# A planner's estimate of TensorE that counts a fixed time for each matrix product

## The chip, the cores and the metric

The kernel runs on one core of one Trainium2 chip. The time is device microseconds from the first to the last instruction of one execution. All weights lie in HBM at the start; the inputs and outputs are those of the reference, in float32.

## The reference

One sequence of 256 tokens with 1024 features goes through two blocks. The first has three residual steps; the second has two layers that carry the tokens and a context stream of 256 rows beside them.

```python
def first_block(...):
    x = x + parallel_mixer(rms_norm(x, mix_norm), w_in, conv_w, lb, hgrn_norm, w_out)
    x = x + memory_cross_attention(rms_norm(x, xattn_norm), rms_norm(mem, mem_norm), w_q, w_kv, w_o)
    x = x + hierarchical_moe(rms_norm(x, ffn_norm), w_group, b_group, w_expert, b_expert, w_gate, w_up, w_down)
    return rms_norm(x, final_norm)

def second_block(x, c, ctx, c_ctx, norm_g, w_ada, ...):
    for l in range(2):
        shift, scale, gate = split(silu(c) @ w_ada[l] + b_ada[l], 3)
        h = rms_norm(x, norm_g[l]) * (1 + scale) + shift
        hc = rms_norm(ctx, norm_g[l]) * (1 + scale_c) + shift_c
        # each of h and hc @ w_in[l]: queries, keys, values of three kinds of attention, z, gates
        o_na, o_mla, o_diff = ...           # the tokens look at tokens and context
        x_new = x + gate * merge_branches(o_na, o_mla, o_diff, z, gm, w_br[l], w_out[l])
        if l == 0:
            ctx = ctx + gate_c * merge_branches(the context's own three branches)
        x = x_new
    return x
```

The router of the mixture of experts takes `softmax(t @ w_group + b_group)` and `t @ w_expert + b_expert` (4 + 16 columns) and picks one of four groups and two of its four experts for each token.

## The kernel before

Most products take float32 operands as two float32r parts: `hi` carries the leading bits, `lo` the rest, and a product of two matrices is three products on TensorE (hi·hi, hi·lo, lo·hi), 128 rows deep and 256 or 512 columns wide. The weights come in units of 512 KB (for instance 4 slices of 128 rows by 256 columns). SP issues the load into a raw tile `w`, ACT copies it into its leading part `wh`, DVE subtracts to make `wl`. A unit of `gemm_t` (token rows out, 256 columns) is 4 slices x 2 token tiles x 3 parts = 24 products for each stream.

The program is one straight list of instructions for each engine. Its order is set while it is built: every part of the computation is a generator (`Fiber`), and `run()` takes, again and again, the fiber that can go on earliest by an estimate, `max(its ready time, self.E["pe"])`, and at equal times the one of the smallest priority number. `self.E` holds the estimated end of each engine's list; `_op` moves it on by a cost, `_pe` computes that cost for products and transposes, `act`, `tt`, `ts`, `stt` do so for ACT and DVE. The estimate also tells `soon()` whether a fiber should let others go first, and `splitter()` when a weight may be split. The build is repeated: the order in which weight units were used in one build is the order in which the next one loads them. On the chip the engines then wait for each other through semaphores, in exactly this order; the estimate itself doesn't run there.

Names that matter below:

- `mm` (line 365) emits a product, `tr` (line 370) a transpose on TensorE against the identity in `csts`; `act` (378) an ACT operation, `tt` (388), `ts` (393, 395), `stt` (400, 402), `red` (407, 409) DVE operations.
- `layer(l, ...)`: one layer of block 2. Its last step, `out`, multiplies the merged branches by `w_out_2` in units of 256 columns and adds them to the tokens' residual `X`: a product with the gate into a temporary `t`, then two additions to `X`. `layers` starts layer 1's context stream as soon as layer 0's context is through (`hidden(C, 1, 1, ...)`); the tokens follow (`rest()`: wait for layer 0, then `hidden(X, 1, 0, ...)`, at the high priority `CRIT`). `hidden` squares and sums `X`, takes the inverse root, scales (one tile on ACT, one on DVE), and `to_T2` makes 16 transposes in four groups and evacuates each group: a scale and shift on DVE or ACT, `hi` on ACT, `lo` on DVE. Layer 1's first projections are 8 units of the context alone; those of the tokens need `hidden`.
- `moe`: the router's logits are products with `wrh`, `wrl` (line 365, 20 rows out), evacuated by ACT (`t<-p,cols 20x256`) and transposed back (`tr`, `p<-csts,t 20x20`). The softmax and the choice follow on DVE.
- `prepare` (priority 8, the lowest): 16 small copies within HBM that lay out the window's bias (`toep`, line 949). ACT's queue issues them, so ACT stands still while an issue lasts.

Of the kernel before, what the change touches and what calls it, by code (L numbers as in the profile page):

```python
# [11 lines left out]
F32R = mybir.dt.float32r  # L12
# [9 lines left out]
EPS = 1e-6  # L22
NEG = -1e30
NE = 16
CAP = 64

# ---------------------------------------------------------------- layout of the packed small operands
# [72 lines left out]
# ---------------------------------------------------------------- program order  # L100
# [5 lines left out]
class Fiber:  # L106
# [10 lines left out]
    def ready(self, eng="pe"):  # L117
        """when the fiber's last result can be used by an engine."""
        return self.t + (0 if self.eng is None else self.SELF[eng] if self.eng == eng else
                         self.HOP_PE if eng == "pe" else self.HOP)  # L120
# [6 lines left out]
class Tiles:  # L127
    """[128, n, w] held as tiles of per entries each."""
# [12 lines left out]
class Core:  # L141
    """Emits the program. Each part of the computation is a generator; run() interleaves them by an
    estimate of when the engines are free, so that one part's products fill another's waits."""
# [3 lines left out]
    # per phase: weights loaded, weights split (each as two parts); the rest of the large tiles are the fibers'  # L147
    WEIGHTS = {"start": (5, 4), "router": (19, 2), "moe": (9, 2), "moe2": (7, 2), "l0": (4, 3), "l1": (3, 4)}
    QUOTA = {"start": {}, "router": {("l", "M"): 3}, "moe": {}, "moe2": {}, "l0": {}, "l1": {}}
    UNITS, OPEN = 6, 5  # L150
    PAR = {1: 1.0, 2: 1.87, 4: 3.6}
# [51 lines left out]
    # ---- generators  # L203
# [47 lines left out]
    # ---- memory  # L251
# [28 lines left out]
    def alloc_t(self, n, w, dt=F32):  # L280
        """[128, n, w] in as many tiles as it takes."""
        per = min(n, 1024 // w)
        ts = []
        for i in range(0, n, per):
            m = min(per, n - i)
            x = yield from self.alloc("M" if m * w > 512 else "S", [128, m, w], dt)
            ts.append(x)
        return Tiles(ts, per)

    def alloc_2(self, n, w):  # L290
        """[128, n, w] twice: leading and trailing parts."""
        hi = yield from self.alloc_t(n, w, F32R)
        lo = yield from self.alloc_t(n, w, F32R)
        return hi, lo
# [12 lines left out]
    def wlimit(self, phase):  # L307
        """the phase's share of the large tiles for weights; what a smaller share gives back is used once it is empty."""
        r, h = self.WEIGHTS[phase]
# [10 lines left out]
    def soon(self, eng="pe"):  # L320
        """other parts first, if what comes would hold up the engine."""
# [16 lines left out]
    # ---- engines  # L338
# [7 lines left out]
    def _pe(self, cycles, rows, par=1.0):  # L346
        """the array runs at its full clock in a tick that follows one with enough columns; par: products side by side."""
# [5 lines left out]
        self._op("pe", cycles * (0.4167 if self.hot else 0.8333) / par)  # L353
# [8 lines left out]
    def mm(self, out, lhsT, rhs, start, stop, par=1.0):  # L362
        n, m = self._n(rhs), self._n(lhsT)
        self._pe(max(n, 2 * m) if rhs.dtype == F32R else max(4 * n, 4 * m), lhsT.shape[0], par)
# [53 lines left out]
    def rsqrt(self, ss, inv_n, n):  # L418
        """1/sqrt(ss*inv_n + EPS) for a [128, n] tile; 1/sqrt(ss) without inv_n."""
# [18 lines left out]
    def hilo(self, hi, lo, src, after=None):  # L438
        """Exact split of src: hi carries its leading bits, lo the rest."""
# [4 lines left out]
    # ---- weights  # L444
# [17 lines left out]
    def _slot(self):  # L462
        """a large tile for weights: the one that was given back first."""
# [10 lines left out]
    def _pump(self):  # L474
        """loads ahead of the products, in the recorded order, as far as the buffers allow."""
# [3 lines left out]
    def splitter(self):  # L479
        """splits ahead of the products; hi: the leading bits of the unit's weights, lo: the rest."""  # L480
# [26 lines left out]
    def wget(self, name, lead, k0, k1, c0, c1, plain=False):  # L507
        """the weights [k0*128:k1*128, c0:c1], [128, k, c]: split, or plain as they are."""
# [66 lines left out]
    def gemm_w(self, name, lead, K, c0, c1, hi, lo, evac):  # L575
        """out[feature, token]: evac(i, psum [128, 2, 256]) for each 256 columns."""
# [19 lines left out]
    def gemm_x(self, name, lead, K, c0, c1, hi, lo, evac, cw=512):  # L596
        """out[token, feature]: evac(i, [psum of tokens 0-127, psum of tokens 128-255], n)."""
# [21 lines left out]
    def gemm_f(self, name, lead, K, c0, blocks, hi, lo, evac, pair=False, base=0, end=2 * T, kev=None):  # L619
        """out[feature, token] in blocks of at most 128 features; blocks: (features, first token), the tokens running to  # L620
        end, of which hi/lo hold those from base; kev: what each entry of hi/lo waits for. evac(block, psum [features, tokens], psum tile), or with pair
        evac(block, psum [128, blocks, tokens], psum tile)."""
# [3 lines left out]
        for b0 in range(0, len(blocks), 2):  # L626
# [12 lines left out]
            for k0 in range(0, kt, 4):  # L639
                w = yield from self.wget(name, lead, k0, k0 + 4, c, c + cw)  # L640
                f = 0
                for j, (fw, t0) in enumerate(bl):
# [4 lines left out]
                    if fw == 32:  # L647
                        # a narrow block's leading and trailing parts side by side, to be added up later
# [4 lines left out]
                        for k in range(4):  # L653
                            # (the product that ends the group writes all of its rows)
# [24 lines left out]
    def gemm_t(self, name, lead, K, c0, c1, hi, lo, streams, evac, cw=256, base=0, kev=None, group=1):  # L679
        """out[token, feature] for both tiles of each stream: evac(i, [psum [128, 2 * cw] for each stream]) for every cw  # L680
        columns; hi/lo hold the tokens from base; kev: what each entry of hi/lo waits for."""
# [31 lines left out]
    def gemm_m(self, name, lead, K, c0, cw, hi, lo, streams, evac, base=0):  # L713
        """out[token, feature], cw columns, the weights held for both tiles of each stream: evac(m, [psum for each stream])."""
# [26 lines left out]
    def gemm_p(self, ps, st, par, units, kt, n=512):  # L741
        """ps[rows of part j] = st(j, k).T @ part j's weights for all parts side by side, the weights as they are;
        units: (name, lead, first column) of each part."""
# [16 lines left out]
    # ---- shared pieces  # L760
# [12 lines left out]
    def norm_rows(self, src, inplace=False):  # L773
        """src / rms, tokens on partitions: two [128, 1024] tiles."""
# [20 lines left out]
    def to_T(self, xs, hi, lo, a=None, b=None, nk=8, at=0, off=0):  # L795
        """transposes xs (two tiles, tokens on partitions) into entries at.. of hi/lo, scaled by columns a, shifted by b."""
# [49 lines left out]
    def add_rows(self, dst, gate=None):  # L846
        """evac for gemm_x: dst += psum (times a gate row)."""
# [14 lines left out]
    # ---- setup  # L862
# [29 lines left out]
    def silu_c(self):  # L892
        """silu of the two conditioning vectors, over and over."""
# [8 lines left out]
    def lower(self):  # L902
        """lower bound of the forget gates: softmax over the layers' rows, its first row."""
# [13 lines left out]
    def prepare(self):  # L917
        """small operands that are needed later: router weights, lambda, the window's bias."""
# [23 lines left out]
        # the window's bias as a function of both columns  # L942
# [12 lines left out]
    # ---- block 1: mixer  # L955
# [195 lines left out]
    def decays(self, A, K, Q, B, KT, qts, made, used):  # L1151
        """level by level: queries and keys times their decays from and to the middle of each block."""
# [29 lines left out]
    # ---- block 1: memory keys and values  # L1182
# [38 lines left out]
    # ---- block 1: cross attention  # L1221
# [78 lines left out]
    # ---- block 1: experts  # L1300
    def moe(self):
# [5 lines left out]
        # router  # L1307
# [96 lines left out]
        # slot numbers of every token as rows, combine weights of every slot as columns  # L1404
# [26 lines left out]
        # tokens beyond an expert's CAP slots, if there are any  # L1431
# [24 lines left out]
    def gained(self, xs):  # L1456
        """the experts' input, tokens on partitions, as leading and trailing parts."""
# [12 lines left out]
    def square(self, m, c):  # L1470
        """the sums of squares of a piece of the residual stream, before and after the final gain."""
# [9 lines left out]
    def gather(self, q, before, hh, hl, pos, C2, cw):  # L1481
        """the rows of four experts' tokens, features on partitions; the slots' weights, two experts side by side."""
# [38 lines left out]
    def experts(self, gat, cw, ups, ys):  # L1521
        """the products with the experts' weights, two experts' slots side by side, one pair after the other."""
        hid = []

        def down(p):
            """the weighted result as leading and trailing parts, slots on partitions."""
# [46 lines left out]
    def hid(self, g, u):  # L1573
        """silu(gate) * up of two experts' slots, features on partitions."""
# [18 lines left out]
    def scatter(self, q, evs, posT, after, piece, pieces):  # L1593
        """token t takes the slots that carry its number."""
# [30 lines left out]
    def overflow(self, hh, hl, over, mxi):  # L1625
        """the dense products of every expert, weighted by over; taken only if an expert's slots ran out."""
# [50 lines left out]
    def final_norm(self, hi, lo):  # L1677
        """the final norm of block 1, and the first layer's norm on top of it: 1/rms of the latter from the sums of squares
        after the gain."""
# [25 lines left out]
    # ---- block 2  # L1705
    def ada(self, l, *evs):
        """shift, scale and gate of layer l for both streams, features on partitions."""
# [42 lines left out]
    def gate_rows(self, l, streams):  # L1750
        """the gates of the streams (0 the tokens, 1 the context) as rows, on every partition."""
# [12 lines left out]
    def hidden(self, src, l, s, hi, lo, inplace=False):  # L1764
        """the modulated, normalised stream s of layer l (0 the tokens, 1 the context) into its half of hi/lo."""
# [10 lines left out]
    def layer(self, l, hi, lo, C, ready, half=None):  # L1776
        """one layer of block 2 on both streams (0 the tokens, 1 the context), the context in columns 0-255 of hi/lo and the
        tokens in 256-511, these from ready on; the last layer takes keys and values alone from the context. The first
        layer has the context alone in hi/lo, which does what it can by itself before the tokens are ready, and half is
        set when the context's residual stream is done."""  # L1780
# [10 lines left out]
        def rope(r, tb, nh, d):  # L1791
            """r [128, m, nh, d] (or [128, m, d], nh None) in place."""
# [19 lines left out]
        def heads(br):  # L1812
            """four tiles of heads, features on partitions, as leading and trailing parts if the scores are taken from these."""
# [15 lines left out]
        def heads_T(raw, np_, nb, dst, d0, gain):  # L1829
            """blocks raw(m, j) of np_ columns, tokens on partitions, into dst[d0 + j]."""  # L1830
# [12 lines left out]
        def sums(n, cols):  # L1843
            """sums of squares of n blocks of columns, to be turned into 1/rms in one go."""
# [3 lines left out]
        def roots(sh, j, inv_n):  # L1848
            """block j's 1/rms, once the other blocks' sums are there too."""
# [868 lines left out]
```

## Time and profile before

| | us |
|---|---|
| median of 3 runs | 1619.11 (1617.6 to 1622.94) |
| span of the profiled execution | 1620.1 |
| PE busy / weight loads busy | 1581.4 / 1333.1 |
| DVE busy / ACT busy | 980.5 / 753.2 |
| mean granted TensorE clock | 0.995 |

PE is TensorE's product side, PEld its weight loads (they run beside the products), DVE the vector engine, ACT the scalar engine. The granted clock is a share of 2.4 GHz; 0.5 is the lower level, 1.2 GHz. In a timeline row the columns are start, duration, engine, line, operation, names out<-in, shape, count, and in brackets the idle time of that engine just before and what ended it. Products overlap in the pipeline, so a row with x2 lasts less than twice a row with x1; the pitch from start to start is what counts.

### The profile page before, as it was taken

To read this page: it belongs to the slowest core of one execution; us is meant where nothing else is said; L and a number is where in the kernel's file an instruction comes from. 1 tells how busy PE (TensorE), PEld (TensorE's weight loads), DVE (VectorE), ACT (ScalarE), POOL (GpSimd) and SP (SyncE) were. 2 spreads that over 40 slices of the span, in tenths; PEclk is the share of its full clock that TensorE was granted. 3 is DMA by queue.
4 is the path that set the end of the run, shared out by engine and by line. 5 is a ranking of instruction groups with operands and counts; after the bars stand their busy time and mean duration, and the time that the engine had idled before them with its cause. 6 is when DMAs were issued, how large, how long until landed. Compare 5 with 4: busy or idle time off the path is not lost.

```text
span 1620.1 us, 28916 instructions
## 1 busy us (share of the span) xinstructions
PE 1581.4 (98%) x11642; PEld 1333.1 (82%) x11642; DVE 980.5 (61%) x2035; ACT 753.2 (46%) x1357; POOL 44.1 (3%) x75
## 2 busy tenths in 40 slices
PE   7999999699999999999999999999999999999998
PEld 6899899663565447998888788888999999989898
DVE  5876557522232246758675463754896776767755
ACT  5535345322522135746653345463464465546652
POOL 0000000000000001011000000000010200000000
PEclk9999999899999999999999999999999999999999
DMA  9667656779998996565314453534755425234441
GB/s 344 225 189 241 221 162 188 237 275 377 383 372 291 353 384 211 170 182 132 104 50 123 128 157 113 166 92 130 234 167 159 118 79 144 69 113 112 144 133 63
DMA packets 233175, 305.31 MB, mean 188 GB/s; under 512 B 17184, under 2 KB 160288, under 8 KB 233040
## 3 DMA queue, kind: packets, MB, share of 16 engines
q1 hardware_dynamic: 222608, 293.11, 56.5%
q0 software_dynamic: 2576, 7.77, 1.7%
q10 hardware_dynamic: 7856, 2.56, 0.8%
q8 instruction: 93, 1.52, 0.4%
q14 instruction: 42, 0.34, 0.1%
HBM read 302.34 MB, written 2.90 MB: 188 GB/s over the span
## 4 chain that ended last, share of the span: by engine, by line
PE 63%; DVE 2%; ACT 1%; DMA 1%; issue 0%; DVEq 0%; ACTq 0%
PE p L365 59%; PE p L370 4%; ACT t L378 1%; DMA w<-in_w_in_dram 1%; DVE t L388 0%; DVE wl L388 0%; DVE t L400 0%; ACT wh L378 0%; DVE t L407 0%; DVE t L409 0%; ACT X L378 0%; DVE t L395 0%; DVE t L393 0%; DVE p L388 0%; DVE X L388 0%
## 5 line engine op out<-in xcount | busy, mean ns | idle before, releaser
L365 PE MATMUL p<-t,wh 128*128 128x256 f32 (+1 forms) x2640 | 560.9, 309 | 0.7 <-DVE t L388 0.7
L365 PE MATMUL p<-wh,t 128*128 128x256 f32 (+2 forms) x2248 | 464.9, 301 | 1.5 <-ACT wh L378 1.2
L388 DVE TENSOR_TENSOR wl<-w,wh 128x1024 fp32r<-128x1024 f32 (+2 forms) x318 | 373.4, 1194 | 133.6 <-ACT wh L378 122.5
L365 PEld LDWEIGHTS p<-t,wh 128*128 128x128 f32 x2640 | 424.1, 190 | 31.0 <-issue 7.8
L378 ACT ACTIVATE t<-p 128x512 f32<-128x512 f32 (+5 forms) x381 | 193.5, 528 | 453.2 <-PE p L365 341.7
L365 PE MATMUL p<-t,wl 128*128 128x256 f32 (+1 forms) x1312 | 399.6, 305 | 0.5 <-DVE wl L388 0.5
L365 PEld LDWEIGHTS p<-wh,t 128*128 128x128 f32 x2248 | 366.3, 192 | 23.9 <-issue 11.0
L378 ACT ACTIVATE wh<-w 128x1024 fp32r<-128x1024 f32 (+2 forms) x318 | 318.7, 1031 | 42.5 <-DMA toep<-in_na_rpb_dram 11.4
L365 PE MATMUL p<-wl,t 128*128 128x256 f32 (+2 forms) x1124 | 335.4, 298 | 2.1 <-DVE wl L388 2.1
L365 PEld LDWEIGHTS p<-t,wl 128*128 128x128 f32 x1312 | 250.0, 191 | 11.8 <-DVE wl L388 0.9
L365 PE MATMUL p<-t,t 128*64 128x128 f32 (+8 forms) x1824 | 244.6, 308 | 3.0 <-DVE t L388 1.3
L365 PEld LDWEIGHTS p<-t,t 128*64 128x64 f32 (+3 forms) x1824 | 195.3, 170 | 51.6 <-issue 27.6
L365 PEld LDWEIGHTS p<-wl,t 128*128 128x128 f32 x1124 | 216.0, 192 | 7.9 <-DVE wl L388 3.0
L378 ACT ACTIVATE t<-p,t 128x512 f32<-128x512 f32 (+3 forms) x232 | 120.0, 555 | 129.7 <-PE p L365 85.6
L365 PE MATMUL p<-w,t 128*64 128x512 f32 x768 | 176.1, 598 | 1.3 <-ACT t L378 0.7
L370 PE MATMUL p<-csts,t 128*128 128x128 f32 (+1 forms) x848 | 119.4, 278 | 12.9 <-ACT t L378 11.9
L365 PEld LDWEIGHTS p<-w,t 128*64 128x64 f32 x768 | 51.4, 136 | 95.7 <-issue 87.5
L370 PEld LDWEIGHTS p<-csts,t 128*128 128x128 f32 (+1 forms) x848 | 96.0, 141 | 31.3 <-ACT t L378 15.6
L388 DVE TENSOR_TENSOR t<-t,t 128x512 f32<-128x512 f32 (+9 forms) x254 | 107.0, 455 | 15.0 <-ACT t L378 12.1
L378 ACT ACTIVATE t<-p,cols 128x256 fp32r<-128x256 f32 (+4 forms) x91 | 50.4, 604 | 127.5 <-PE p L370 74.8
L407 DVE TENSOR_REDUCE t<-p 128x1 f32<-128x512 f32 (+1 forms) x124 | 85.0, 685 | 40.3 <-PE p L365 39.0
L400 DVE SCALAR_TENSOR_TENSOR t<-t,p 128x512 f32<-128x512 f32 x70 | 47.8, 684 | 72.2 <-ACT t L378 38.8
(95 smaller groups left out, 684.8 us busy)
## 6 DMA issues: line engine op xcount, KB each, us to landing
w<-in_w_in_dram SPq DMA_DIRECT2D x206, 512.0 KB, 4.4
w<-in_w_gate_dram SPq DMA_DIRECT2D x64, 512.0 KB, 8.5
w<-in_w_up_dram SPq DMA_DIRECT2D x64, 512.0 KB, 10.3
w<-in_w_down_dram SPq DMA_DIRECT2D x64, 512.0 KB, 10.7
w<-in_w_ada_dram SPq DMA_DIRECT2D x48, 512.0 KB, 4.5
w<-in_w_out_dram SPq DMA_DIRECT2D x32, 512.0 KB, 3.9
w<-in_w_br_dram SPq DMA_DIRECT2D x28, 512.0 KB, 4.4
w<-in_w_kv_dram SPq DMA_DIRECT2D x16, 512.0 KB, 4.1
```

The costliest lines, as they stand in the source:

```text
L365: self.nc.tensor.matmul(out, lhsT, rhs, start=start, stop=stop)
L370: self.nc.tensor.transpose(out, in_, self.ident[:k, :k])
L378: self.nc.scalar.activation(out, in_, func, bias=bias, scale=scale, **kw)
L388: self._e(eng, self._n(out), False, after).tensor_tensor(out, a, b, op=op)
L400: e.scalar_tensor_tensor(out, a, s, b, op0=op0, op1=op1)
L407: e.tensor_reduce(out, a, axis=AX, op=op, negate=True)
```

## The change

`_pe` gets a fourth argument, a fixed time in nanoseconds that it adds to the estimate of each call. `mm` passes 13.5 for a float32r product and 6 for another; a transpose gets 3. The rest of the diff deletes comments, so lines move by four (365 becomes 369, 949 becomes 953).

```diff
     UNITS, OPEN = 6, 5
+    PEF, PEX = 13.5, 3.0
     PAR = {1: 1.0, 2: 1.87, 4: 3.6}
...
-    def _pe(self, cycles, rows, par=1.0):
+    def _pe(self, cycles, rows, par=1.0, fixed=3.0):
         tick = max(self.E["pe"], self.cur.ready()) // 3413.33
...
-        self._op("pe", cycles * (0.4167 if self.hot else 0.8333) / par)
+        self._op("pe", cycles * (0.4167 if self.hot else 0.8333) / par + fixed)
...
     def mm(self, out, lhsT, rhs, start, stop, par=1.0):
         n, m = self._n(rhs), self._n(lhsT)
-        self._pe(max(n, 2 * m) if rhs.dtype == F32R else max(4 * n, 4 * m), lhsT.shape[0], par)
+        if rhs.dtype == F32R:
+            self._pe(max(n, 2 * m), lhsT.shape[0], par, self.PEF)
+        else:
+            self._pe(max(4 * n, 4 * m), lhsT.shape[0], par, 2 * self.PEX)
         self.nc.tensor.matmul(out, lhsT, rhs, start=start, stop=stop)
```

No instruction is added or removed: PE's list has 9142 rows before and after. The order moves on all engines, in many places by a few rows. Names in the rows below carry the number of a buffer's use (`wh_11911`, `p_11992`), and these differ between the two programs.

First place, PE, from layer 0's last step to layer 1's tokens, before. `p_11992` is the last 256 columns of the tokens' `w_out_2`, `p_12081` and `p_12142` (48 products each) and `p_12244`, `p_12329` behind them are layer 1's context projections, the rows at L370 the tokens' transposes:

```order
L365 MATMUL p_11992<-wl_11912,t_11337 128x256
L365 MATMUL p_11992<-wh_11911,t_11338 128x256
L365 MATMUL p_12081<-wh_11976,t_11732 128x256
...
L365 MATMUL p_12142<-wl_12107,t_11735 128x256
L365 MATMUL p_12142<-wh_12106,t_11739 128x256
L370 MATMUL p_12205<-csts,t_12063 128x128
L370 MATMUL p_12205<-csts,t_12064 128x128
...
L365 MATMUL p_12244<-wh_12136,t_11732 128x256
```

The same place now: `p_12237` is the last of the eight context units, `p_11997` the last `w_out_2` unit (24 products), `p_12382` the first of the four groups of the tokens' transposes, `p_12429` the first projection of the tokens:

```order
L369 MATMUL p_12237<-wl_12231,t_11734 128x256
L369 MATMUL p_12237<-wh_12230,t_11738 128x256
L369 MATMUL p_11997<-wh_11946,t_11303 128x256
L369 MATMUL p_11997<-wl_11947,t_11303 128x256
...
L369 MATMUL p_11997<-wh_11946,t_11341 128x256
L374 MATMUL p_12382<-csts,t_12348 128x128
L374 MATMUL p_12382<-csts,t_12349 128x128
...
L369 MATMUL p_12429<-wh_12262,t_11731 128x256
```

All eight context units now stand ahead of the last `w_out_2` unit, and between that unit, the tokens' transposes and the tokens' first projection there is nothing else on PE.

Second place, ACT, around the router's logits, before (`t_3014` is the router's input, `toep` the copies of `prepare`, `t_3212` the logits):

```order
L378 ACTIVATE t_3014<-p_3172,cols 128x256 x2
L378 ACTIVATE t_3014<-p_3182,cols 128x256 x2
L378 ACTIVATE t_3083<-t_3087 128x1024
L378 ACTIVATE t_2980<-p_3090 128x2x256
L949 DMA toep_2807<-in_na_rpb_dram 7x64x64 x5
L378 ACTIVATE t_3212<-p_3064,cols 20x256
```

And now (`t_2978` is the router's input, `t_3216` the logits):

```order
L382 ACTIVATE t_2978<-p_3130,cols 128x256 x2
L382 ACTIVATE t_2978<-p_3139,cols 128x256 x2
L382 ACTIVATE t_3031<-t_3084 128x1024
L382 ACTIVATE t_2813<-p_3148,cols 128x512
L382 ACTIVATE wh_3161<-w_2804 128x1024
L382 ACTIVATE t_2813<-p_3156,cols 128x512
L953 DMA toep_2810<-in_na_rpb_dram 7x64x64 x6
L382 ACTIVATE wh_3195<-w_2844 128x1024
L382 ACTIVATE t_3216<-p_3015,cols 20x256
```

The burst has six issues instead of five, two evacuations and a split stand ahead of it that did not, and another split stands between it and the logits. On PE, 8 transposes (`p_3148`, `p_3156`) and a unit of 24 products now stand between the router's last transposes and its last products, where nothing stood; behind those products both programs have 24 products and then the logits' two transposes.

Third place, ACT behind the tokens' transposes at the layer boundary now (`p_12390` and `p_12407` are the second and fourth group of transposes, `t_11731` and `t_11732` the leading parts):

```order
L382 ACTIVATE t_12349<-X,t_12353 128x1024
L382 ACTIVATE t_12395<-p_12390,adaab_10369 128x256 x2
L382 ACTIVATE t_11731<-t_12387 128x2x256
L382 ACTIVATE t_11732<-t_12395 128x2x256
L382 ACTIVATE t_12413<-p_12407,adaab_10369 128x256 x2
```

Before, ACT evacuated both of its groups first and made the leading parts later; now the first two leading parts come between them.

## Rows read from the trace of the kernel before

**Rows 1.** The page's busy shares: engine, busy us, share of the span, instructions.

```profile
PE 1581.4 (98%) x11642; PEld 1333.1 (82%) x11642; DVE 980.5 (61%) x2035; ACT 753.2 (46%) x1357; POOL 44.1 (3%) x75
```

**Rows 2.** PE's waits: line waited for, us in total, times, longest; 12 rows.

```profile
PE p L370 <- ACT t L378: 11.9, 5, 8.9
PE p L365 <- DVE t L393: 11.0, 1, 11.0
...
PE p L365 <- PEq L1637: 0.2, 1, 0.2
```

**Rows 3.** Stretches: length, busy us (instructions) of PE, PEld, DVE, ACT, POOL; clock, DMA.

```profile
1193.00:1204.50 11.50, 11.50 (x98) 11.50 (x97) 10.98 (x23) 6.58 (x8) 0.00 (x0) 1.00 0.75 238
307.50:311.00 3.50, 3.49 (x17) 3.45 (x18) 2.58 (x11) 1.96 (x3) 0.00 (x0) 0.51 0.43 106
```

**Rows 4.** The page's groups of weight splits: busy us, mean ns of one.

```profile
L388 DVE TENSOR_TENSOR wl<-w,wh 128x1024 fp32r<-128x1024 f32 (+2 forms) x318 | 373.4, 1194 | 133.6 <-ACT wh L378 122.5
...
L378 ACT ACTIVATE wh<-w 128x1024 fp32r<-128x1024 f32 (+2 forms) x318 | 318.7, 1031 | 42.5 <-DMA toep<-in_na_rpb_dram 11.4
```

**Rows 5.** Timeline of DVE, 1194 to 1209 us, the tokens' residual and norm.

```profile
1194.03 0.68 DVE L388 TENSOR_TENSOR t<-p,t 128x512 f32<-128x512 f32 x1
1194.75 0.76 DVE L388 TENSOR_TENSOR X<-t,X 128x256 f32<-128x256 f32 x2
1195.54 1.23 DVE L402 SCALAR_TENSOR_TENSOR t<-X 128x1024 f32<-128x1024 f32 x1
...
1196.88 0.37 DVE L395 TENSOR_SCALAR t<-t 128x2 f32<-128x2 f32 x2
...
1198.66 0.36 DVE L400 SCALAR_TENSOR_TENSOR t<-t,t 128x2 f32<-128x2 f32 x2
...
1205.15 1.90 DVE L395 TENSOR_SCALAR t<-p,adaab 128x256 f32<-128x256 f32 x4 [0.33 <-PE p L370]
```

**Rows 6.** Timeline of ACT, same stretch.

```profile
1200.39 1.14 ACT L378 ACTIVATE t<-X,t 128x1024 f32<-128x1024 f32 x1
...
1205.58 1.93 ACT L378 ACTIVATE t<-p,adaab 128x256 f32<-128x256 f32 x4 [3.10 <-PE p L370]
...
1208.82 0.65 ACT L378 ACTIVATE t<-t 128x512 fp32r<-128x512 f32 x1
```

**Rows 7.** Timeline of PE, the tokens' transposes at the layer boundary.

```profile
1204.51 1.91 PE L370 MATMUL p<-csts,t 128*128 128x128 f32 x16
1206.17 0.36 PE L365 MATMUL p<-wh,t 128*128 128x256 f32 x1
```

**Rows 8.** Timeline of PE, the tokens' transposes ahead of layer 0.

```profile
664.19 1.91 PE L370 MATMUL p<-csts,t 128*128 128x128 f32 x16
...
668.80 0.39 PE L365 MATMUL p<-wh,t 128*128 128x256 f32 x1
...
669.53 0.51 PE L365 MATMUL p<-wh,t 128*128 128x256 f32 x2 [0.22 <-DVE t L388]
```

**Rows 9.** Timeline of ACT, the router's logits.

```profile
294.51 0.76 ACTq L949 DMA_DIRECT2D toep<-in_na_rpb_dram  x1
...
295.85 11.09 ACTq L949 DMA_DIRECT2D toep<-in_na_rpb_dram  x4
306.99 0.46 ACT L378 ACTIVATE t<-p,cols 20x256 f32<-20x256 f32 x1 [11.28 <-DMA toep<-in_na_rpb_dram]
```

**Rows 10.** All `toep` issues: ns shortest/median/longest, first and last start in us.

```profile
L949 ACTq DMA_DIRECT2D toep<-in_na_rpb_dram x16: 755/807/5102, 242.6 to 304.5; - x16
```

**Rows 11.** Timeline of PE around the router's logits.

```profile
292.07 1.04 PE L370 MATMUL p<-csts,t 128*128 128x128 f32 x8
...
294.12 0.30 PE L365 MATMUL p<-t,wrh 128*20 128x256 f32 x1 [0.59 <-DVE t L400]
...
...
307.51 0.40 PE L370 MATMUL p<-csts,t 20*128 20x20 f32 x2 [8.93 <-ACT t L378]
```

**Rows 12.** Timeline of PE, the heads' transposes of the cross attention.

```profile
234.28 1.35 PE L370 MATMUL p<-csts,t 128*128 128x128 f32 x8 [1.19 <-ACT t L378]
```

## The prediction

> **What bounds the kernel now.** I read four views in this order: the busy shares, the waits of PE, the busy time by stretch, and the timelines of the places where the change moves work. The profiled span is 1620.1 us and PE is busy for 1581.4 us of it [rows 1], so all of PE's waits together can't be more than some 39 us; the view of waits names 33.6 us in twelve rows, from 11.9 down to 0.2 us [rows 2]. 11.0 us of that is the start, before any product. The router's stretch, 290 to 330 us, has five waits from 8.93 down to 0.59 us, 12.5 us in sum (these two in [rows 11]). What is left, 33.6 - 11.0 - 12.5 = 10.1 us, lies in small pieces over the rest of the span. Everywhere else PE is the bound by its own work.
>
> That work can't change here. The products are the same before and after; only their order differs. So the time moves by waits alone: those that the new order closes (at most 10.1 + 12.5 us, since the start is the same) and those that it opens. I therefore went through PE's new order and looked for places where work that used to cover a dependence has gone.
>
> Is the estimate's new constant right? 96 products of 256 columns take 11.52 us, 120 ns apiece (the stretch from 1193 us, with 98 rows, two of them the end of what stood ahead [rows 3]). 256 columns at 2.4 GHz are 106.7 ns, so 13.3 ns come on top, and the estimate of before, without a constant, ran ahead of PE by 12%. The new 13.5 ns fits. But a planner that is right on average may still choose a worse order at one place, because it is greedy: it takes what can start now, and doesn't look at what will be missing later.
>
> The Trainium skill, "TensorE: Matmul & The Clock Gate", section "Wait — 56ns, not 53.3ns?", speaks against the new constant: it finds a fixed 2.5 ns behind each warm product, not 13.5. By that a unit of 24 products would be 2.62 us and the old estimate the better one; these rows show 2.88 us, so the measurement decides. Were the page right, the first rival below would lose its ground, and the router's term would be 0.3 us larger, since the unit moved there would cover less.
>
> **The layer boundary: +10.6 us.** Before, the last unit that completes the tokens' residual of layer 0 (`w_out_2`, columns 768 to 1023) ends at about 1193.0. Four units of layer 1's context projections follow (the 96 products, 11.52 us) [rows 3], then the 16 transposes of the normalised tokens at 1204.51, and other context units right behind these [rows 7]. The work between the residual and the transposes therefore costs PE nothing: no wait is recorded there. In the new order all eight context units stand ahead of the last `w_out_2` unit; the transposes stand directly behind it and the tokens' own products directly behind these. Nothing is left to cover the chain. Its links, one by one: the product of gate and sum 0.68, the two additions to X 0.76, the square with its sum 1.23, the small operations of the inverse root from 1196.88 to 1199.02 2.14 [rows 5], the scaling on ACT 1.14 [rows 6]; together 5.95. In the new order no weight split stands between them on DVE, so I leave out what lies before the scaling now, from 1199.02 to 1200.39. Three hops between engines and the end of the last product add some 0.75 (an estimate from the 0.33 us that the transposes' evacuation waits for PE, where the other hops in these rows are 0.02 to 0.1 [rows 5]). Sum 6.7 us without PE.
>
> Then the transposes and what comes behind them. PE falls to the lower of its two clocks, 1.2 GHz, after such a wait: behind the 8.93 us wait the granted clock was 0.51 for 3.5 us, and 17 products took 3.49 us, 205 ns apiece instead of 120 [rows 3]. So the first four transposes, 0.42 us of the 1.66 that the 16 take before [rows 7], take 0.8. Their evacuation waits 0.33 and takes half of 1.90 on DVE; ACT evacuates the next four, half of 1.93, and in the new order makes the leading half of the first tile directly behind them, 0.65 [rows 5, 6]. With hops the first product can start 3.8 us behind the first transpose, and it takes 0.4 more until the trailing half is there: 4.2 - 1.66 = +2.5. The nearest other site, the tokens' norm at 664.19, needs 5.0 us from the first transpose to steady products, 4.61 to the first of them and 0.4 in them [rows 8]; that would be +3.3. Last, some 17 products at the lower clock: +1.4. Sum 6.7 + 2.5 + 1.4 = **+10.6 us**. Bounds: below, if hops are short and the clock is back with the transposes, 8; above, by the other site and with two splits of 1.2 us [rows 4] in between after all, 14. I take 10.6, since its links are read at this very site.
>
> **The router: +2.6 us.** Around 300 us ACT issues five DMAs (`toep`, line 949) and is held by them from 294.51 to 306.94: the first takes 0.76, the other four 11.09 together, and the last, issued at 304.5, still takes 2.4 [rows 9, 10]. The router's logits wait behind them for 11.28 us, and PE behind the logits for 8.93 us [rows 9, 11]. Counted from the first transpose of the router's second half (292.07), PE runs out of other work at 6.5 us and goes on at 15.4, and there is a wait of 0.59 before that: 9.5 us in all. In the new order ACT does its four evacuations and the large scaling as before (to 3.1 us), then two more evacuations (0.65 each, as the same size in rows 6) and a split (1.03 [rows 4]): 5.4. The burst has six issues now: 11.9 + 2.4 = 14.3, to 19.7. One more split, 1.03, stands ahead of the logits, 0.46: 21.1. PE has 24 products and 8 transposes (2.9 and 0.9 us) more ahead of the router's last products and so runs out at 8.9 (the 0.59 wait is covered), and waits 12.1 us: 12.1 - 9.5 = **+2.6**. Bounds: -2 (a burst that starts before those evacuations, while PE's cover has grown) to +5 (an issue of 5 us, the longest in that row, among the six).
>
> **Cross attention: +1 us.** The new order puts three `w_kv` units between the four heads' transposes; they cover the 1.19 us wait at 234.28 [rows 12], but then the first head's product waits for the values' evacuation that ends right before it: between 0 and +2.5, I take +1 net.
>
> **All the rest: 0, between -4 and +4.** The other waits are 10.1 us in small pieces; the order changes at most of them and I see no rule by which they close or open.
>
> **The sum**: 1620.1 + 10.6 + 2.6 + 1 = 1634.3 us for a profiled execution. The profiled span before lies 1.0 us above the median of the runs (1619.11), so the median should be 1633.3; I say 1633.
>
> **The rivals.** *No change.* The better estimate closes the small waits: 10.1 us outside start and router are there to be won, and of the router's five waits the 3.0 us that I have left alone (12.5 - 8.93 - 0.59) [rows 2, 11]. For it speaks that the constant fits the rows; against it that every such wait has a cause of its own on ACT or DVE, which a PE constant doesn't touch. It decides from 9.3 us won elsewhere (14.2 less the 4.9 us that count as no change); with all 13.1 won the profiled time would be 1634.3 - 13.1 = 1621.2, the median 1620.2: not slower. Chance 0.13.
>
> *The router gets better.* If the DMA queue has room and all six issues take 0.76 us as the first does, the burst takes 4.6 us instead of 14.3, the router's wait falls from 9.5 to 12.1 - 9.7 = 2.4 us, and the sum is 1620.1 + 10.6 + 1 - 7.1 = 1624.6, median 1623.6: about at the edge of what counts as no change. Against it: before, the other four took 2.8 us apiece [rows 9], and the burst has only grown. Chance 0.07.
>
> *The hole is wider.* The splits that run ahead of layer 1's weights get in between after all, or the second pair of transposes is evacuated late as well: +3 to +6 on top, 1637 to 1642. Chance 0.12; beyond 1643, 0.05.
>
> *The change doesn't do what it says.* If the constant were too small to turn a choice, the order would stay and the time with it. The order shows otherwise on all engines, so this has no chance of its own.
>
> **How the numbers follow.** Forecast (1628 to 1637) 0.60, wider hole 0.12, beyond 0.05, router better 0.07, no change 0.13, faster than 1614 by gains that I don't see 0.03. A measurement of this kernel can tell about 0.3%, 4.9 us, from no change. Slower by more than that: 0.60 + 0.12 + 0.05 + 0.03 (half of the router's case) = 0.80; same 0.13 + 0.04 = 0.17; faster 0.03. The range from 1622 to 1643 leaves out most of "no change" (0.10), the faster cases and those beyond: 0.18.
>
> **What would show it.** Right: a wait of PE of 6 to 8 us for ACT ahead of 16 transposes a little after 1200 us, with the lower clock behind it, and the eight context units ahead of it without a wait; a `toep` burst of six issues and a router wait of 10 to 13 us; the sum of PE's waits up by 12 to 15 us while its count of products stays. Wrong: a gap at the boundary under 4 us, which would mean the chain was priced from links that overlap; a router wait under 7 us; or small waits elsewhere whose sum falls by more than 5 us.

## The result, and the profile after

| | before | after |
|---|---|---|
| device time, median | 1620.55 us (4 runs, 1617.6 to 1622.94) | 1636.23 us (4 runs, 1634.12 to 1638.06) |
| ratio after / before | | 1.0096, 95% interval 1.0084 to 1.0109 |
| span of the profiled execution | 1620.1 us | 1632.2 us |
| device time of that same execution | 1621.99 us | 1634.12 us |

The change makes the kernel 15.7 us (1.0%) slower. The two profiled executions lie only 12.1 us apart: the one of before is the second slowest of its four, the one of after the fastest of its four. All readings below are of these two, so they explain 12.1 us; the other 3.6 us are scatter between runs. A device time stands about 2 us above its span here, so the 1.0 us by which I set the profile of before above the median compared two different things. Both traces hold 11642 rows of PE.

First the view of PE's waits after (line waited for, us in total, times, longest). It answers to [rows 2]; lines are four higher now.

```profile
PE p L369 <- DVE sil L416: 10.7, 1, 10.7
PE p L374 <- ACT t L382: 10.5, 5, 8.3
PE p L374 <- DVE t L397: 7.0, 3, 6.0
PE p L369 <- DVE t L392: 6.6, 4, 4.1
PE p L374 <- DVE t L392: 5.0, 4, 1.8
PE p L369 <- DVE wl L392: 3.8, 3, 2.6
```

The start (10.7) and the wait for ACT in the router's stretch (8.3) are old. New are a wait of 6.0 us for the scaling at line 397 and one of 4.1 us for a DVE product at line 392. They are in the places where the order has changed.

Both programs hold the same products, so I cut both at the same work and took from each stretch the number of products times their pitch at full clock (120 ns for 256 columns, and so on). What is left over is what PE loses there, and only the difference between the two kernels counts: start to 60 us +2.6; mixer and cross attention -1.8; router -0.3; experts and layer 0 -1.2; **layer boundary +9.0**; layer 1 to about 1440 us +0.2; from there to the end +3.8. The sum is +12.3, the spans differ by 12.1. Not every difference of this size means something: e1 below has the changed kernel's order on PE up to the layer boundary and loses 17.5 us in the router, where the changed kernel loses 16.0. So below some 1.5 us two executions differ by scatter, and the router's -0.3 and the -1.2 of the experts are no differences.

**The layer boundary.** PE after, the tokens' transposes and the first of the tokens' own products (start, us, what; in brackets the idle time before). It answers to [rows 7].

```profile
1222.26 3.77 PE L374 MATMUL p<-csts,t 128*128 128x128 f32 x16 [5.96 <-DVE t L397]
1225.95 0.58 PE L369 MATMUL p<-wh,t 128*128 128x256 f32 x1
```

And the stretch from 1222 us (busy us and instructions of PE, PEld, DVE, ACT, POOL; then granted clock, DMA share, GB/s):

```profile
1222.00:1226.00 4.00, 3.74 (x17) 3.30 (x17) 1.90 (x5) 2.15 (x5) 0.00 (x0) 0.50 0.00 0
```

The transposes wait 5.96 us and then run at the lower clock, 3.77 us instead of 1.91. The chain that they wait for, on DVE after (it answers to [rows 5]):

```profile
1216.33 0.69 DVE L392 TENSOR_TENSOR t<-p,t 128x512 f32<-128x512 f32 x1
1217.06 0.76 DVE L392 TENSOR_TENSOR X<-t,X 128x256 f32<-128x256 f32 x2
1217.85 1.22 DVE L406 SCALAR_TENSOR_TENSOR t<-X 128x1024 f32<-128x1024 f32 x1
1219.00 0.08 DVE L406 DVE_READ_ACCUMULATOR t<-X 128x1 f32 x1
1219.19 0.37 DVE L399 TENSOR_SCALAR t<-t 128x2 f32<-128x2 f32 x2
...
1221.36 0.75 DVE L397 TENSOR_SCALAR t<-X,t 128x1024 f32<-128x1024 f32 x1
```

Link by link it is the chain that the prediction added up: evacuation, residual, square, inverse root, scaling, one directly behind the other, with no weight split between. Only the last link is another: PE starts when the tile scaled on DVE (0.75 us) is there, while ACT's tile takes 1.15.

**The router.** ACT after, from the evacuation of the router's last transposes to its logits (ACTq rows are issues by ACT's queue; it answers to [rows 9]):

```profile
289.78 1.57 ACT L382 ACTIVATE t<-p,cols 128x256 fp32r<-128x256 f32 x4 [3.17 <-PE p L374]
291.10 0.76 ACTq L953 DMA_DIRECT2D toep<-in_na_rpb_dram  x1
...
292.69 3.10 ACTq L953 DMA_DIRECT2D toep<-in_na_rpb_dram  x1
292.74 1.08 ACT L382 ACTIVATE wh<-w 128x1024 fp32r<-128x1024 f32 x1
...
295.83 9.20 ACTq L953 DMA_DIRECT2D toep<-in_na_rpb_dram  x3
305.07 1.06 ACT L382 ACTIVATE wh<-w 128x1024 fp32r<-128x1024 f32 x1 [10.68 <-DMA toep<-in_na_rpb_dram]
306.04 0.45 ACT L382 ACTIVATE t<-p,cols 20x256 f32<-20x256 f32 x1
```

The six issues take 13.9 us, from 291.10 to 305.03. But the first three run while ACT's operations ahead of them in the list are still at work, so the burst ends 15.9 us after the router's last transposes begin (289.14), and PE's wait there is 8.3 us, 0.6 less than in [rows 11].

### The profile page after: what moved, and what is told of

The parts are those of the page before. It is cut to its first block, busy times and chain, and to the rows that moved or that the text cites. A ratio compares the mean times of both kernels' runs of the same rounds, so it can differ in the third digit from the quotient of the medians.

```text
span 1632.2 us, 28915 instructions
## 1 busy us (share of the span) xinstructions
PE 1581.0 (97%) x11642; PEld 1335.6 (82%) x11642; DVE 980.1 (60%) x2035; ACT 753.7 (46%) x1357; POOL 42.8 (3%) x75
## 5 line engine op out<-in xcount | busy, mean ns | idle before, releaser
L382 ACT ACTIVATE wh<-w 128x1024 fp32r<-128x1024 f32 (+2 forms) x318 | 318.5, 1032 | 35.1 <-DMA toep<-in_na_rpb_dram 12.3
L369 PE MATMUL p<-t,t 128*64 128x128 f32 (+7 forms) x1824 | 238.9, 308 | 1.8 <-DVE t L416 1.0
```

The source lines that it names most:

```text
L369: self.nc.tensor.matmul(out, lhsT, rhs, start=start, stop=stop)
L382: self.nc.scalar.activation(out, in_, func, bias=bias, scale=scale, **kw)
```

## Experiments

Nine kernels, each beside runs of the kernel before on the same chip (medians 1620.1 to 1620.8 us there). The changed kernel was not run again beside them, so a difference of 1 us to its 1636.2 means nothing. "PE's loss" is the measure of the section above.

| run | median, us | ratio to before, interval |
|---|---|---|
| e1, layer 1 behind at ties | 1626.38 | 1.0030 (1.0016 to 1.0045) |
| e2, 13.5 ns for split products only | 1640.64 | 1.0122 (1.0105 to 1.0139) |
| e3, 6 and 3 ns for the rest only | 1622.08 | 1.0011 (1.0001 to 1.0020) |
| e4, bias copies by GpSimd | 1635.26 | 1.0096 (1.0079 to 1.0114) |
| e5, 13.0 ns instead of 13.5 | 1639.18 | 1.0114 (1.0097 to 1.0131) |
| e6, e1 and copies by GpSimd later | 1621.10 | 1.0005 (0.9992 to 1.0019) |
| e7, before, copies by GpSimd later | 1613.01 | 0.9954 (0.9937 to 0.9970) |
| e8, e1 without constants in layer 1 | 1624.97 | 1.0037 (1.0018 to 1.0056) |
| e9, before, constants in layer 1 | 1623.18 | 1.0016 (1.0006 to 1.0026) |

**e1: is the hole the order's doing?** In `run()` a fiber of equal time and equal priority wins by age. Layer 1's context stream and layer 0's last step both have priority 3, and the stream is older.

```diff
         self.spawn(rest(), prio=self.CRIT, name="hidden")
+        self.cur.prio += 0.5
         yield from self.layer(1, hi, lo, None, x1)
```

> The changed kernel, with layer 1's context stream one half priority step behind layer 0's last step, so that a tie goes to the tokens' residual; then the last w_out_2 unit and the tokens' transposes stand again ahead of four of the eight context units. Theory (the hole at the layer boundary is opened by the order of these units alone): PE's wait of 6.0 us ahead of the 16 transposes and the slow clock behind it go, the time falls by about 9 us against the changed kernel, to 1627 (profiled 1623). Rival (the lost time only moves, because the constant starves something behind it): the wait comes back within layer 1 and the time stays at 1634 to 1637.

Measured 1626.4 us, 9.8 less than the changed kernel. PE from 1185 to 1210 us, where the tokens' norm now stands:

```profile
1185.00:1210.00 25.00, 25.00 (x212) 25.00 (x211) 22.58 (x40) 14.60 (x22) 8.32 (x12) 1.00 0.64 193
```

PE is busy for all 25 us at full clock, and its loss at the boundary is 0.0 instead of 9.0. So the order of these units makes the hole: with the last `w_out_2` unit and the tokens' transposes ahead of four context units it is gone, and the wait doesn't come back elsewhere. Why the constant opened it can be read from the planner's code and its estimate; no run isolates this step. In the estimate of before DVE lags behind PE, so layer 1's stream, whose input comes through DVE and ACT, isn't ready when the tokens' last unit comes up, and that unit goes first although its fiber is the younger. With PE estimated 13% slower DVE no longer lags, both fibers are ready "now" at each of the eight units, and age decides for the stream, unit after unit.

**e2 and e3: which of the constants?** e2 keeps 13.5 ns for split products and sets the others to 0, e3 the other way round.

```diff
-    PEF, PEX = 13.5, 3.0
+    PEF, PEX = 13.5, 0.0
...
-    def _pe(self, cycles, rows, par=1.0, fixed=3.0):
+    def _pe(self, cycles, rows, par=1.0, fixed=0.0):
```

> The changed kernel, but the fixed time counts for the split products alone (13.5 ns); plain products and transposes count none, as before the change. Theory (the 13.5 ns turn the ties at the layer boundary): the last w_out_2 unit stands behind all eight context units as in the changed kernel, the 6 us wait is there, slower than before by 8 to 15 us. Rival (the transposes' and plain products' share opens the waits): the time goes back to within 4 us of before.

> The changed kernel, but split products count no fixed time, as before the change; plain products count 6 ns and transposes 3 ns. Theory: the layer boundary keeps the order of before, no 6 us wait there, time within 4 us of before. Rival (the transposes' share opens the waits): slower by 8 us or more.

Measured 1640.6 and 1622.1 us. e3's order at the boundary is that of before and it loses nothing there; e2's is that of the changed kernel, with the wait of 6.0 us. So the 13.5 ns do it. e2 is 4.4 us slower still than the whole change, outside what I expected: the constant that it leaves out, though it is small, turns other choices. Its waits between 335 and 1100 us (the first two of that view):

```profile
PE p L369 <- DVE wl L392: 4.8, 2, 3.9
PE p L374 <- DVE t L392: 3.3, 3, 1.8
```

A wait of 3.9 us for a weight split stands there that neither the kernel before nor the changed one has.

**e5: is it how well the estimate fits?** 13.0 ns is as near as 13.5 to the 13.3 ns of [rows 3].

```diff
-    PEF, PEX = 13.5, 3.0
+    PEF, PEX = 13.0, 3.0
```

> The changed kernel with 13.0 ns instead of 13.5 for a split product. That is as close to the 13.3 ns of the rows as 13.5 is, but at the layer boundary it makes another order: both halves of the last w_out_2 pair first, then all eight context units, then the tokens' transposes and their own products. Theory (the order there sets the time, not how well the estimate fits): the norm's chain is covered by 23 us of products and only the transposes' evacuation is open, so the boundary loses 2 to 3 us instead of 9; time 1628 to 1632. Rival (the time follows the calibration): 13.0 and 13.5 agree within 3 us, 1634 to 1638.

Measured 1639.2 us: not what I expected of the order, and above the rival's range too, though within its 3 us of the changed kernel (2.95). On PE's list the last `w_out_2` unit stands ahead of all eight context units, which looks like 23 us of cover. The trace shows a wait all the same. PE, then DVE:

```profile
1229.99 3.82 PE L374 MATMUL p<-csts,t 128*128 128x128 f32 x16 [4.77 <-DVE t L397]
```

```profile
1202.08 0.76 DVE L392 TENSOR_TENSOR X<-t,X 128x256 f32<-128x256 f32 x2
...
1222.74 1.41 DVE L404 SCALAR_TENSOR_TENSOR t<-p,cols,t 128x512 fp32r<-128x512 f32 x2 [1.22 <-ACT t L382]
1224.26 1.22 DVE L392 TENSOR_TENSOR wl<-w,wh 128x1024 fp32r<-128x1024 f32 x1
1225.40 1.22 DVE L406 SCALAR_TENSOR_TENSOR t<-X 128x1024 f32<-128x1024 f32 x1
```

The residual is done at 1202.84, but the square that follows starts at 1225.40. It stands in DVE's list behind the evacuations of the last context units, because the fiber of layer 0's last step, which had nothing left to do but to end, lost its ties against the context stream as well, and the norm waits for that end. Cover on PE's list is worth nothing when the chain that it should cover stands late in another engine's list. PE's loss at the boundary is 8.1 us, about that of the change; against the changed kernel it loses 3.0 us more in the router, 2.9 more among the experts and layer 0 and some 3 more ahead of the router, and less in layer 1. I had read only PE's order for this expectation. Since the boundary loses as much as with 13.5, for another reason, this run doesn't decide between the theory and its rival; that the order sets the time rests on e1.

**e4: what is ACT's queue worth in the router?** The 16 copies go by GpSimd's queue, which has little to do.

```diff
-                nc.scalar.dma_start(
+                nc.gpsimd.dma_start(
                     d[:, h].rearrange("c (r k) -> r c k", r=7),
```

> The changed kernel, with the 16 copies of the window's bias issued by GpSimd's queue instead of ACT's. Theory (ACT's queue held by six issues keeps the router's logits back): the 8.3 us wait of PE ahead of the logits' transposes falls below 1 us, and with the slow clock behind it about 9 to 11 us are won: 1625 to 1628. Rival (the softmax's DVE chain or the memory behind it would hold PE at the same place anyway): less than 4 us won.

Measured 1635.3 us, 1 us less than the changed kernel; by the rival's number the rival wins, but not by its reason. The wait ahead of the logits' transposes is gone, and PE's loss in the router falls from 16.0 to 5.6 us. In the stretch ahead of it the loss rises from 4.1 to 11.7. PE, then ACT, then GpSimd:

```profile
245.37 4.70 PE L369 MATMUL p<-t,t 128*128 128x256 f32 x14 [5.91 <-ACT t L382]
```

```profile
235.99 0.93 ACTq L928 DMA_DIRECT2D t<-in_lrows_dram  x1
236.11 0.59 ACT L382 ACTIVATE t<-p 128x512 f32<-128x512 f32 x1
244.50 0.34 ACT L382 ACTIVATE wrh<-t 128x160 fp32r<-128x160 f32 x1 [7.80 <-DMA t<-in_wr_dram]
```

```profile
230.92 5.73 POOL L953 DMA_DIRECT2D toep<-in_na_rpb_dram  x7 [0.69 <-DMA toep<-in_na_rpb_dram]
```

GpSimd hardly waits between the copies and issues fifteen of the sixteen from 223.4 to 236.7 us, just as ACT loads the router's weights. These 80 KB now land 8.9 us after their issue (1.9 in the kernel before, 4.1 in e6 below, where the copies come later), ACT waits 7.8 us for them at the head of its list (0.8 in the changed kernel, 3.0 in e6), and PE waits for the evacuation behind.

**e6 and e7: the same copies, later.** GpSimd first multiplies a small tile that is ready only after the router's weights. e6 adds this to e1, e7 to the kernel before.

```diff
+        z = yield from self.alloc("T", [128, 4])
+        nc.gpsimd.tensor_tensor(z, lt, lt, op=OP.mult)
+        self.free(z)
         self.free(lt)
...
-                nc.scalar.dma_start(
+                nc.gpsimd.dma_start(
```

> The changed kernel with layer 1's context stream behind at ties, and with the 16 bias copies issued by GpSimd's queue, which first multiplies a small tile by itself that is ready only after the router's weights have landed. Theory (both waits are ACT's queue and the order at the boundary; the 5.9 us wait that came up when GpSimd issued the copies at 229 us was the router's weights arriving late behind them): no wait of PE above 2 us between 240 and 335 us, about 9 to 11 us less than with the boundary mended alone, 1615 to 1619. Rival (the copies crowd out the weight loads wherever they run): a new wait for a weight split or DMA of 4 us or more between 240 and 300 us, 1620 to 1625.

> The kernel before with the 16 bias copies issued by GpSimd's queue in the same way, behind the small multiplication. Theory: the 8.9 us wait and the slow clock behind it go, 9 to 12 us less than before: 1609 to 1612, the fastest of all. Rival (as for the changed kernel, a new wait takes their place): 1616 to 1621.

Measured 1621.1 and 1613.0 us. e7's waits of PE from 240 to 335 us:

```profile
PE p L365 <- DVE wl L388: 2.3, 2, 1.2
PE p L365 <- ACT wh L378: 1.3, 1, 1.3
PE p L370 <- DVE t L409: 0.6, 1, 0.6
PE p L365 <- DVE t L400: 0.6, 1, 0.6
```

No wait is longer than 1.3 us where 8.9 stood, and the router's loss falls from 16.3 to 7.4 us. **e7 beats both kernels** (0.46% under before). Its gain is 7.1 us by the medians, less than the 9 to 12 I expected. In e6 the router's loss falls by 11.7 us (17.5 to 5.8), its waits there are at most 1.8 us, and the profiled spans of e1 and e6 differ by 9.3; the medians differ by 5.3, with e6's ten runs spread from 1615.0 to 1623.2. So e6 supports the theory by its waits and shows none of the rival's, but its median lies in the rival's range. The rest is scatter: the profiled execution of e6 lies 2.9 us below its median, that of e1 1.5 above. In e6 the time goes with TensorE's granted clock, from 1615.0 us at 0.997 to 1623.2 at 0.991.

**e8 and e9: the wait in layer 1.** The constants switch at the moment the tokens' norm of layer 1 is through: in e8 they end there, in e9 they begin there.

```diff
         r, h = self.WEIGHTS[phase]
+        if phase == "l1":
+            self.PEF, self.PEX = 0.0, 0.0
...
```

> The changed kernel with layer 1's context stream behind at ties, and the fixed times set to zero from the moment the tokens' norm of layer 1 is through. PE's order up to the layer boundary is then that of the kernel with the boundary mended, and from there on that of the kernel before. Theory (the 4.1 us wait near 1511 to 1522 us is made by layer 1's own order): that wait goes, 3 to 4 us less than with the boundary mended alone (1626.4), 1622 to 1623.5. Rival (layer 1 inherits its wait from what stands before): the wait stays, 1625 to 1628.

> The kernel before up to the layer boundary, with no fixed time, and 13.5, 6 and 3 ns from the moment the tokens' norm of layer 1 is through. PE's order is that of the kernel before up to there and, but for a few rows, that of the changed kernel behind. Theory (layer 1's own order makes the wait): a wait of about 4 us for DVE near 1505 to 1515 us, 3 to 4 us more than before, 1623 to 1625. Rival: as before within 2 us, 1618.5 to 1622.

Measured 1625.0 and 1623.2 us. PE from 1480 us on, the longest wait in e8 and in e9:

```profile
1508.91 2.08 PE L372 MATMUL p<-t,t 96*128 96x256 f32 x4 [1.28 <-DVE t L395]
```

```profile
1513.96 0.69 PE L372 MATMUL p<-wh,t 128*128 128x384 f32 x1 [4.12 <-DVE t L395]
```

The 4.1 us wait goes with layer 1's own order, not with what stands before it: gone in e8, there in e9, on the same product as in the changed kernel. In the changed order the 12 transposes and 20 products of the attention run ahead of the last `w_uq_2` unit, which is then left alone behind a chain on DVE; before, 12 transposes and 12 products stood inside that unit. In time it is worth 2.4 us (e9 against before) and 1.4 (e8 against e1; its runs spread from 1622.5 to 1632.3, so this one is unclear), less than the 3 to 4 I expected, since before has smaller waits in the same place. By time alone e9 lies in its theory's range and e8 just below its rival's.

e8 also shows what a part of the scatter is. The kernel before has the same order here and the same wait of 1.28 us on the same four products, yet these last 1.13 us there, at a granted clock of 1.00, and 2.08 in e8, at 0.50 (1509 to 1511 us). Ahead of them PE had waited 1.2, 0.4 and 1.3 us within 6 us in both. Over e8's seven runs the granted clock goes from 0.994 at 1622.5 us to 0.989 at 1632.3.

## Why the prediction was right, point by point

**The time.** 1633 was forecast, 1636.2 came, inside 1622 to 1643, and slower as forecast. In the profiled pair the forecast was +14.2 and +12.1 came; two terms of the sum had the wrong sign, and 5.4 us that I had put at nothing made up for them. That the sum came so near is luck; that the boundary is the largest term is not. Of the signs that I named, the boundary's wait (5.96 us for 6 to 8, but for DVE and not ACT), the six issues and the sum of PE's waits (up by 12.3 us) came, the router's wait of 10 to 13 us didn't (8.3).

**The layer boundary: the mechanism right, the size 9.0 for 10.6.** The chain without PE: 5.96 us measured for 6.7. I had led it through ACT's scaling (1.14); with DVE's, which PE waits for, the links are 5.55, and the hops 0.41 where I had 0.75. From the first transpose to the first of the tokens' products 3.69 us were measured for 3.8. What comes behind, the trailing half and the products at the lower clock, costs 0.9 instead of 0.4 + 1.4: the granted clock was 0.50 from 1222 to 1227 us, most of it under the transposes, and 1.00 from 1228 on, so a few products ran slowly and not 17. e1 shows the term as a whole: 9.8 us come back.

**The router: wrong, -0.3 for +2.6.** The burst itself was well priced (13.9 us for 14.3) and has six issues as read from the order. The step that failed is its start. I let it begin when the evacuations and the split ahead of it in ACT's list were over, 5.4 us after the transposes; it began after 2.0. In these traces ACT's queue issues while operations ahead of it in the list still run (the split at 292.74 beside the issue at 292.69); only what stands behind an issue waits for it. The trace of before had this to see, in a row ahead of [rows 9] that I hadn't weighed: the first issue starts at 294.51 while this scaling is still running.

```profile
294.15 1.08 ACT L378 ACTIVATE t<-t 128x1024 fp32r<-128x1024 f32 x1
```

The sum has a slip besides: its own terms let PE run out of work at 9.7 us (6.5 - 0.59 + 2.9 + 0.9) and not at 8.9, which would have made the term +1.9; measured were 9.1.

**Cross attention: wrong, about -1.8 for +1** (with the mixer). The three `w_kv` units cover the 1.19 us wait of [rows 12], as read; the wait for the values' evacuation that I set against it does not appear: the products behind the last of these transposes start at once. That the -1.8 is no scatter shows in e1 and e8, which lose as little there, and in e7 and e9, which lose as much as before.

**All the rest: +5.4 where I had 0 between -4 and +4.** 3.8 of it is the end of layer 1 with its wait of 4.1 us, which e8 and e9 tie to the constant's order there; it could have been found in the order as the boundary was, by looking for a unit that has lost what stood between it and its norm. 2.6 is the start, where a split waits for a weight load. PE's list is the same there in all kernels, so it is the order of the loads and splits: where it is that of the changed kernel (e1, e4, e6, e8 and itself) PE waits 1.4 to 3.0 us for splits between 18 and 48 us, where it is that of before (e7 and itself) 0.2 to 0.8. e2, with the changed loads but the splits in the order of before, loses nothing there against before (15.9 for 16.0), and e5 loses 3.9. Which load or split it is no run isolates.

**The rivals.** *No change*, because the better estimate closes small waits: what was won is 3.3 us (mixer and cross attention, router, experts), only the first 1.8 of it more than scatter, and what was lost elsewhere is more. With the boundary mended (e1) the constant is still 5.6 us slower than before. *The router gets better*: by 0.3, not by 7; its issues were as slow as before. *The hole is wider*: no.

## What to carry to other kernels

A greedy list scheduler doesn't get better merely because one of its costs gets truer. Here it was decided by who wins when two things are ready at the same time, and a truer cost turned accidents of readiness into ties that age decided. Give the work at the head of a long chain a priority that says so, then tune costs. And read the order of every engine on the chain, not only of the one that will wait: cover counts only if the chain's own operations stand early in their lists.

## What the runs showed of the hardware

The time on top of a split product's columns is nearly the same at 256 and 512 columns, and it is there at the higher clock only. In the kernel before, 156 split products of 512 columns take 35.49 us from 1086.15 us on, at a granted clock of 1.00: 227.5 ns apiece, 14 more than the columns (213.3), as the 13.3 at 256 columns. PEld is busy for 29.4 of these 35.49 us, so it isn't the weight loads that set the pitch. After the router's wait PE is at the lower clock (granted 0.50), and in the changed kernel three products of 256 columns start every 0.64 us:

```profile
307.82 0.63 PE L369 MATMUL p<-wh,t 128*128 128x256 f32 x2
308.25 0.41 PE L369 MATMUL p<-wl,t 128*128 128x256 f32 x1
308.46 0.63 PE L369 MATMUL p<-wh,t 128*128 128x256 f32 x2
```

That is 213 ns apiece, 256 columns at 1.2 GHz (213.3) with nothing on top, against 120.0 at the higher clock, where 106.7 would be the columns alone. The Trainium skill, "TensorE: Matmul & The Clock Gate", section "Wait — 56ns, not 53.3ns?", says the same of the lower clock; its 2.5 ns for the higher one is not what these split float32r products show (13.3).

The issue of a copy within HBM of 112 KB costs ACT 0.76 us when it is among the first of a burst and up to 5.2 us behind others; GpSimd takes 0.82 to 0.90 us for each of the 16 (e4, e6, e7), back to back or not.
